# One subtraction moved behind another group, and one product split by halves of k instead of by columns, in a two-level fast matrix product

## The chip, the cores and the metric

The kernel runs on 1 core of one Trainium2 chip. The metric is device time in microseconds (us) for one execution. The kernel before takes 1524.74 us, the median of 3 runs (1524.18 to 1525.29).

Engines are named as in the profile: PE is TensorE (matmuls; PEld its weight loads), DVE is VectorE, ACT is ScalarE, POOL is GpSimd, SP is SyncE. L12 is line 12 of the kernel before.

## The reference

```python
m, k, n = 4096, 4096, 4096          # a, b, bias in float32
return np.tanh(np.matmul(a, b) + bias)
```

## The kernel before, in words

**Products.** The kernel does not multiply plainly. It works on items. An item is one column chunk `c` of 1024 columns (four chunks) and one pair of 128-row blocks of `a` (sixteen pairs). With the two row blocks, the two halves of k and the two halves of the chunk's columns, each item is a 2 x 2 by 2 x 2 block product, and seven products `m1` to `m7` stand in for eight: `m2 = s2 b11`, `m5 = s5 b22`, `m3 = a11 d3`, `m1 = s1 d1`, `m4 = a22 d4`, `m6 = s6 e6`, `m7 = s7 e7`. The left operands `s` are differences of quarters of `a` (`s6 = a21 - a11`, `s1 = a22 - a11`), the right operands `d` and `e` are sums and differences of quarters of `b`, all in fp16. A whole product is 16 matmuls (16 tiles of 128 along k) of 512 columns.

**Two levels.** In chunks 1 to 3, two items share a second level of the same idea: for a product such as m4, the two items' left operands, each cut into halves of k, are again a 2 x 2 block, and seven small products of 8 matmuls and 256 columns replace eight. The results of the small products are put together in PSUM by VectorE sums, with one ScalarE copy (`third`, L885) of a PSUM half to SBUF in between.

**The four-product order.** From some item on, chunks 2 and 3 treat two items `p` and `q` at a time in `four` (L992), which does m4, m2, m3 and one or two of m5 and m6 on two levels and m1, m7 whole. The order is written out by hand, and every engine takes its instructions in the order of the calls. For a pass that does not leave the order ("not leave"; `leave` is the last pass of chunk 2) TensorE's order is:

- m4 group 0, m2 group 0, m4 group 1, m2 group 1, m4 group 2, m2's products 7 and 3;
- m3 group 0, m2's product 4, x group 0, m3 group 1, x group 1, m3 group 2, x product 7 (x and y are m6 and m5, or m5 and m6);
- m1 of q, whole (16 matmuls of 512 columns);
- x products 3 and 4, y group 0;
- m1 of p, the columns 0 to 255 (16 matmuls, L1227);
- y group 1;
- m1 of p, the columns 256 to 511 (16 matmuls, L1230);
- y products 7 and 3, m7 of p, y product 4, m7 of q.

`group0` (L888), `group1` (L901) and `single` issue the small products through `multiply` (L868; the matmul is L879); `whole` (L935; the matmul is L939) issues a whole product. `group0` of m4 returns a function, called `w` in `four`, that does one VectorE sum: it adds the copy `x` of one PSUM half and another half into the place where m4's group 1 will accumulate. `group1` of m4 returns one that does two such sums, which m4's group 2 needs. `left` (L827) makes one small left operand on VectorE (128 x 1024), `four_sum` (L944) one whole left operand (128 x 2048); both end in `tt` (L144), so all VectorE arithmetic has line L144 in the profile. `seed` (L973) is a ScalarE copy of zeros into PSUM.

**Entering the order.** `turn_over` (L1311) runs once for chunk 2 and once for chunk 3, ahead of their first pass. It issues the last products of the two items before, while VectorE makes the first operands of the new pair `m`, `m + 1`. It ends with s6 of `m` (L1367), the last two products, s6 of `m + 1` (L1381) and one seed on ScalarE (L1383). Both s6 are written over a21. In later passes, `four` makes s6 of its items itself (L1087, L1112). The first use of the second item's s6 is the operand `v1` of m6, made after m2's products 7 and 3 (L1124).

**Right operands from memory.** Half-size right operands of m2 and m6 ("form") come back from device memory: each time TensorE has used one, `let_go` frees its tile and `pull_four` (L805) issues the next transfer on POOL's queue. Quarters of `a` are fetched on SP's queue.

Of the kernel before, what the change touches and what calls it, by code (L numbers as in the profile page):

```python
# [12 lines left out]
T = 16  # L13
TB = 4
TP = T // 2
# [87 lines left out]
HALF = (ds(0, NB // 2), ds(NB // 2, NB // 2))  # L103
# [10 lines left out]
def kernel(  # L114
# [28 lines left out]
    def tt(out_, in0, in1, op):  # L143
        nc.vector.tensor_tensor(out=out_, in0=in0, in1=in1, op=op)  # L144
# [6 lines left out]
    def bank(n, s, what):  # L151
        two = items[n][2] is not None
        if what == "w":
            return banks[5 + 2 * (n % 2)]
        if what == "z":
            return banks[4 + 2 * (n % 2) + (s if two else 0)]
        return banks[(0 if what == "d" else 2) + (s if two else n % 2)]
# [157 lines left out]
    def by_four(x):  # L315
        return x if len(x.shape) == 4 else x.rearrange("p (a b) m -> p a b m", b=TB)
# [507 lines left out]
    def half_of(n, what, h):  # L824
        return by_four(aset[n][TWO[what][0]])[:, ds(h * TP // TB, TP // TB)]

    def left(n, what, name):  # L827
        if what in FOURTH:
            left_of_four(n, what, name)
            return  # L830
        (i, h), (j, g) = {
            "s2": ((1, 0), (1, 1)), "s5": ((0, 1), (0, 0)), "s1": ((1, 1), (0, 0)),
            "s6": ((1, 0), (0, 0)), "s7": ((0, 1), (1, 1)),
        }[name]
        tt(by_four(place_for(what, name)), half_of(n + i, what, h), half_of(n + j, what, g), SUB)

    def place_for(what, name):
        k = left_count[0] % 4
        left_count[0] += 1
        owner[k] = what, name  # L840
        placed[what, name] = lefts[k]
        return lefts[k]

    def left_of_four(n, what, name):
        of = {"v2": "v1", "v4": "v2"}.get(name)
        if of:
            assert (what, of) in owner.values()
            of = by_four(placed[what, of])
        place = by_four(place_for(what, name))
        if name == "v1":  # L850
            tt(place, half_of(n + 1, what, 0), half_of(n + 1, what, 1), SUB)
        elif name == "v2":
            tt(place, half_of(n, what, 0), of, SUB)
        elif name == "v3":
            tt(place, half_of(n + 1, what, 0), half_of(n, what, 0), SUB)
        else:
            tt(place, half_of(n, what, 1), of, SUB)
# [30 lines left out]
    def group0(n, what, swapped=False):  # L888
        p, q = pair_of(n, what)
        if what in FOURTH:  # L890
            multiply(n, what, p[:, HALF[0]], (0, 0), (0, 0))
            nc.scalar.copy(p[:, HALF[1]], p[:, HALF[0]])
            multiply(n, what, between(n, what), "v1", "t1")
            return lambda: None
        parts = [(p[:, HALF[1]], "s5", (1, 1)), (q[:, HALF[0]], "s2", (0, 0))]
        for part in reversed(parts) if swapped else parts:
            multiply(n, what, *part)
        x = third(q[:, HALF[0]])
        return lambda: tt(between(n, what), x, p[:, HALF[1]], ADD)
# [32 lines left out]
        multiply(n, what, p[:, HALF[0]], "s7", "e7")  # L932
        multiply(n, what, q[:, HALF[1]], "s6", "e6")

    def whole(n, left_, right, parts=None, anew=False):  # L935
        at = by_four(aset[n][left_])
        for to, half in parts or ((bank(n, 0, "z"), ds(0, NB)),):
            for t in range(T):
                nc.tensor.matmul(  # L939
                    to[:, half], at[:, t // TB, t % TB], bop[right, t // TB][:, t % TB, half],  # L940
                    start=anew and t == 0, stop=t == T - 1, skip_group_check=True,
                )

    def four_sum(n, name, there):  # L944
        x, y = {
            "s2": ("a21", "a22"), "s5": ("a12", "a11"), "s1": ("a22", "a11"),
            "s6": ("a21", "a11"), "s7": ("a22", "a12"),
        }[name]
        st = aset[n]
        if there in QUADS:  # L950
            st[name] = st[there]
        elif there in "AB":
            st[name] = side[:, :, ds(NB * "AB".index(there), NB)].rearrange("p a (b m) -> p a b m", m=P)
        else:
            pool = {"wide": wide, "sum": sums, "spare": spare}.get(there, bops)
            st[name] = pool.tile([P, T, P], fp16, name=name, tag="sum" if there == "spare" else there)
        tt(by_four(st[name]), by_four(st[x]), by_four(st[y]), SUB)
# [29 lines left out]
    def more(calls):  # L987
        for f in left_over[:-(-len(left_over) // calls)]:
            f()
            left_over.pop(0)  # L990

    def four(n):  # L992
        c = items[n][0]
        p, q, m = n, n + 1, n + 2
        first, last = n == begins[c], m == len(items)
# [21 lines left out]
        def forms_at(k):  # L1017
            if first:
                m5_forms(k)

        def step(k):
            if leave:
                give_back(c, k)
# [12 lines left out]
        def take(what, i, later=False):  # L1036
            to = bank(i, 0, mine[what])
            if what == "m6":
                tt(st[i]["o"], st[i]["o"], to, ADD)
                ready = ("o", i, 1, 1)  # L1040
            else:
                tt(st[i]["ds"], st[i]["ds"], to, SUB)
                tt(st[i]["s"], to, st[i]["s"], ADD)
                ready = ("s", i, 0, 1)
            if later:
                left_over.append(lambda: end(*ready))
            else:
                end(*ready)
# [26 lines left out]
        left(n, "m2", "v2")  # L1075
        group0(n, "m2")
        left(n, "m4", "s7")
        more(3)
        step(1)
        w = group1(n, "m4")  # L1080
# [143 lines left out]
            fetch(m, "a22")  # L1224
            fetch(m + 1, "a22")
        forms_at(9)
        whole(p, "s1", "d1", ((bank(p, 0, "z"), HALF[0]),))  # L1227
        w, w2 = group1(n, y)
        take(x, q)
        whole(p, "s1", "d1", ((bank(p, 0, "z"), HALF[1]),))  # L1230
        if not last:
            fetch(m, "a11")
        w()
# [77 lines left out]
    def turn_over(c):  # L1311

        m = begins[c]
        p, q = m - 2, m - 1
        left_count[0] = 0
        del free[:]

        def slot(at):
            for f, args in work.pop(SLOTS * p + at, ()):
                if f in (put_four, put_sum, put_block):  # L1320
                    f(*args)

        queue.extend(
            (what, f) for n in range(m, ends_with[c], 2) for what in ("m2", "m6") for f in FOUR
            if what == "m2" or n + 2 in fours or c == NC - 1
        )
        free.extend(("b11_1", "b11_2", "b11_3"))
        for i in range(3):
            pull_four()
        aset[q]["s6"] = side[:, :, ds(0, NB)].rearrange("p a (b m) -> p a b m", m=P)  # L1330
        tt(aset[q]["s6"], by_four(aset[q]["a21"]), by_four(aset[q]["a11"]), SUB)
        asum(q, "s1")
        asum(q, "s7")
        fetch(m, "a22")
        fetch(m + 1, "a22")
        fetch(m, "a11")
        fetch(m + 1, "a21")
        slot(8)
        product(p, *PRODUCTS[8])
        fetch(m, "a21")  # L1340
        fetch(m + 1, "a11")
        product(q, *PRODUCTS[2])
        left(m, "m4", "s5")
        m5_forms(-7)
        slot(9)
        slot(10)
        twice(p, "m4", 2)
        left(m, "m4", "s2")
        seed(m, "d", 1)
        seed(m + 1, "d", 0)  # L1350
        m5_forms(-6)
        product(q, *PRODUCTS[5])
        slot(12)
        m5_forms(-5)
        four_sum(m, "s2", "sum")
        slot(13)
        product(p, *PRODUCTS[10])
        m5_forms(-4)
        seed(m, "z", 0)
        four_sum(m + 1, "s2", "sum")  # L1360
        left(m, "m2", "v1")
        seed(m, "c", 0)
        seed(m, "c", 1)
        slot(15)
        m5_forms(-3)
        if S6_AT == 0:
            four_sum(m, "s6", "a21")  # L1367
        product(q, *PRODUCTS[8])
        free.extend(("e6_2", "e6_3"))
        for i in range(2):  # L1370
            pull_four()
        slot(17)
        m5_forms(-2)
        if S6_AT == 1:
            four_sum(m, "s6", "a21")
        product(q, *PRODUCTS[10])
        free.append("sum")
        pull_four()
        if S6_AT == 2:
            four_sum(m, "s6", "a21")  # L1380
        four_sum(m + 1, "s6", "a21")  # L1381
        m5_forms(-1)
        seed(m + 1, "c", 0)  # L1383

# [219 lines left out]
    first = new_sum([P, 4, 4, TB * QP], fp16, "first")  # L1604
# [153 lines left out]
    for c in range(1, NC):  # L1758
        n = next(n for n in range(len(items)) if items[n][0] == c)
# [4 lines left out]
    for c in TWICE:  # L1764
# [31 lines left out]
        if c < NC - 1:  # L1796
            s1 = SLOTS * max(n for n in partner if items[n][0] == c)
# [43 lines left out]
    for slot in range(1 - len(ORDER), SLOTS * len(items)):  # L1841
# [14 lines left out]
        for pos, p in PRODUCTS.items():  # L1856
            n, r = divmod(slot - pos, SLOTS)
# [37 lines left out]
```

## Time and profile before

| | |
|---|---|
| median of the runs | 1524.74 us |
| profiled execution, device time | 1523.57 us |
| its span in the trace | 1521.9 us |
| granted TensorE clock | 1.00 |
| entry into the four-product order, chunk 2 / chunk 3 | about 928 us / 1251 us |
| passes that reach L1227 and L1230 | 3 in chunk 2, 6 in chunk 3 |

The profile is of one execution. Its span runs from the first to the last instruction; the device time also holds what lies around it. In a timeline row the columns are start and duration in us, engine, line, operation, output and inputs, and the number of instructions merged into the row; in brackets, how long the engine was idle before it and what released it. The matmuls are pipelined, so a row's duration holds the tail of its last matmul, and the distance from one row's start to the next row's start is what a step costs TensorE. The chain of waits follows the work that ended last back from the end; its rows give start, duration, engine and line.

### The profile page before, as it was taken

Reading aid. Unit: us, or ns where it says so; the run is one execution under the profiler, and the core shown is the slowest. Engines: PE = TensorE matmul, PEld = TensorE weight load, DVE = VectorE, ACT = ScalarE, POOL = GpSimd, SP = SyncE. Lnnn points to the kernel's source line nnn. Section 1 sums busy time; section 2 is a strip of 40 time slices with the busy share of each in tenths; the row PEclk is TensorE's granted clock in tenths of the full one; section 3 lists DMA queues with packets and bytes.
Section 4 is the critical chain, followed back from the end, with each engine's and each line's share of the span. In section 5 each row is a group of like instructions: output and inputs, shape, how many; then the busy total and the mean of one; then the engine's idle time right before and its main releaser. Section 6 shows DMA issues by size and latency. Waiting matters only on the chain.

```text
span 1521.9 us, 23593 instructions
## 1 busy us (share of the span) xinstructions
PE 1516.1 (100%) x8925; PEld 872.4 (57%) x8925; DVE 1238.9 (81%) x1671; ACT 347.6 (23%) x729; POOL 477.5 (31%) x868
## 2 busy tenths in 40 slices
PE   9999999999999999999999999999999999999999
PEld 4444444444445666544444557777644558878777
DVE  6789877777987777777798878988769979888887
ACT  4432111111221122111122112222122222223222
POOL 8775443333503231344560222111112211111110
PEclk9999999999999999999999999999999999999999
DMA  9999999999979998999996889889966789888884
GB/s 187 182 209 260 282 234 214 229 211 227 188 214 296 263 284 265 237 258 234 228 187 189 293 272 327 308 296 317 347 227 194 224 278 328 316 307 296 308 289 159
DMA packets 207254, 386.69 MB, mean 254 GB/s; under 512 B 25250, under 2 KB 104354, under 8 KB 207140
## 3 DMA queue, kind: packets, MB, share of 16 engines
q0 software_dynamic: 117232, 198.50, 56.6%
q1 hardware_dynamic: 89236, 186.36, 35.6%
q8 instruction: 70, 1.15, 0.3%
q10 hardware_dynamic: 672, 0.33, 0.1%
q14 instruction: 44, 0.36, 0.1%
HBM read 330.83 MB, written 139.98 MB: 309 GB/s over the span
## 4 chain that ended last, share of the span: by engine, by line
PE 99%; DVE 0%; DMA 0%; ACT 0%; issue 0%; DVEq 0%
PE ps L467 58%; PE ps L879 19%; PE ps L939 10%; PE ps L662 6%; PE ps L1540 5%; DMA coarse<-in_a_dram 0%; PE warm L1600 0%; DVE a L144 0%; PE spread L430 0%; PE tp L1641 0%; DVE form L144 0%; DVE h L144 0%; DVE o L144 0%; DVE first L1636 0%; DVE ps L144 0%; ACT ds L1269 0%
## 5 line engine op out<-in xcount | busy, mean ns | idle before, releaser
L467 PEld LDWEIGHTS <-s 128*128 128x128 f16 x2160 | 211.3, 98 | 249.6 <-DVE s L144 0.2
L467 PEld LDWEIGHTS <-a 128*128 128x128 f16 x1920 | 187.9, 98 | 223.5
L467 PE MATMUL ps<-b,s 128*128 128x512 f16 x1148 | 262.0, 379 | 0.0
L467 PE MATMUL ps<-e,a 128*128 128x512 f16 x908 | 206.9, 379 | 0.0
L467 PE MATMUL ps<-d,a 128*128 128x512 f16 x896 | 202.5, 379 | 0.0
L144 DVE TENSOR_TENSOR s<-a,a 128x2048 f16<-128x2048 f16 (+1 forms) x148 | 177.9, 1205 | 19.5 <-DMA a<-scratch 18.2
L269 DVE STREAM_TRANSPOSE a<-nat 128x1024 f16<-128x1024 f16 (+2 forms) x202 | 175.0, 910 | 9.8 <-PE ps L467 8.3
L879 PEld LDWEIGHTS <-h 128*128 128x128 f16 x1696 | 165.9, 98 | 24.8 <-DVE h L144 0.8
L811 POOL DMA_DIRECT2D form<-form_m x133 | 70.4, 529 | 348.5 <-PE ps L879 318.8
L467 PE MATMUL ps<-d,s 128*128 128x512 f16 x656 | 148.3, 379 | 0.0
L144 DVE TENSOR_TENSOR a<-a,a 128x2048 f16<-128x2048 f16 x120 | 145.7, 1215 | 0.0
L241 POOL DMA_DIRECT2D nat<-in_a_dram x176 | 93.0, 533 | 133.9 <-DVE a L269 63.4
L370 POOL DMA_DIRECT2D b<-in_b_dram x192 | 103.4, 545 | 82.5 <-DVE a L269 31.1
L879 PE MATMUL ps<-form,h 128*128 128x256 f16 x752 | 95.7, 273 | 0.0
L491 ACT ACTIVATE o<-ps 128x512 f32<-128x512 f32 x90 | 54.1, 601 | 163.2 <-issue 92.9
L939 PEld LDWEIGHTS <-a 128*128 128x128 f16 x608 | 58.9, 98 | 34.6
L879 PE MATMUL ps<-d,h 128*128 128x256 f16 x640 | 76.4, 273 | 0.0
L144 DVE TENSOR_TENSOR ps<-ps,x 128x256 f32<-128x256 f32 x126 | 53.8, 428 | 25.0 <-PE ps L879 10.0
L144 DVE TENSOR_TENSOR h<-a,a 128x1024 f16<-128x1024 f16 x108 | 71.5, 681 | 0.0
L939 PE MATMUL ps<-e,a 128*128 128x512 f16 (+2 forms) x320 | 68.8, 368 | 0.0
L662 PEld LDWEIGHTS <-h 128*128 128x128 f16 x600 | 58.7, 98 | 14.7
L879 PEld LDWEIGHTS <-a 128*128 128x128 f16 x600 | 58.7, 98 | 8.7
(186 smaller groups left out, 1933.5 us busy)
## 6 DMA issues: line engine op xcount, KB each, us to landing
a<-scratch SPq DMA_DIRECT2D x140, 512.0 KB, 5.5
form<-form_m POOLq DMA_DIRECT2D x133, 512.0 KB, 6.1
out_dram<-o SPq DMA_DIRECT2D x222, 256.0 KB, 5.6
nat<-in_a_dram POOLq DMA_DIRECT2D x288, 128.0 KB, 7.1
scratch<-a SPq DMA_DIRECT2D x48, 512.0 KB, 6.7
b<-in_b_dram POOLq DMA_DIRECT2D x160, 128.0 KB, 5.7
scratch<-a SPq DMA_DIRECT2D x32, 256.0 KB, 6.1
cast<-in_b_dram POOLq DMA_DIRECT2D x64, 128.0 KB, 9.0
```

Of the source, the lines that this page charges most:

```text
L144: nc.vector.tensor_tensor(out=out_, in0=in0, in1=in1, op=op)
L241: nc.gpsimd.dma_start(out=tl[ds(q * QP, QP), :, :], in_=src.rearrange("(mb p) k -> p mb k", p=QP),)
L269: nc.vector.transpose(dst[:, ds(b0 * tb, n * tb), :].rearrange("P (b t) (mb p) -> P mb b t p", t=tb, p=QP), src[:, :, ds(b0, n), :].rearra ...
L370: nc.gpsimd.dma_start(out=dst[ds(q * QP, QP), ds(t, nt)], in_=src)
L467: nc.tensor.matmul(st[where], at, bt, start=(what == "m2" or n < LEAD and what == "m1") and i == 0, stop=i == len(ts_) - 1, skip_group_che ...
L491: nc.scalar.activation(o, src, TANH)
L662: nc.tensor.matmul(to, at, bt, start=False, stop=t == TP - 1, skip_group_check=True)
L811: nc.gpsimd.dma_start(out=rights[what, name], in_=forms[what, name])
L879: nc.tensor.matmul(to, at, bt, start=False, stop=t == TP - 1, skip_group_check=True)
L939: nc.tensor.matmul(to[:, half], at[:, t // TB, t % TB], bop[right, t // TB][:, t % TB, half], start=anew and t == 0, stop=t == T - 1, skip ...
L1540: nc.tensor.matmul(mb[m % 4, j], aq[m, kt // T][:, kt % T, :], right(kt, j), start=fresh and kt == k0, stop=stop and kt == k1 - 1, skip_gr ...
```

## The change

Three edits in two functions. (1) `turn_over` no longer makes s6 of the second item. (2) The first pass of `four` makes it, after the second small operand that follows m4's group 0 and m2's group 0 and ahead of m4's group 1: `make("s6", q)` is the same `four_sum` over a21. (3) `whole` takes the tiles of k that it is to do, and the first item's m1 is cut at k instead of at the columns: the first 8 tiles of k over all 512 columns ahead of y's group 1, the other 8 behind it. `TP` is 8, `T` is 16.

```diff
-    def whole(n, left_, right, parts=None, anew=False):
+    def whole(n, left_, right, parts=None, anew=False, steps=range(T)):
         at = by_four(aset[n][left_])
         for to, half in parts or ((bank(n, 0, "z"), ds(0, NB)),):
-            for t in range(T):
+            for t in steps:
                 nc.tensor.matmul(
                     to[:, half], at[:, t // TB, t % TB], bop[right, t // TB][:, t % TB, half],
                     start=anew and t == 0, stop=t == T - 1, skip_group_check=True,
...
         left(n, "m4", "s7")
+        if first:
+            make("s6", q)
         more(3)
         step(1)
         w = group1(n, "m4")
...
         forms_at(9)
-        whole(p, "s1", "d1", ((bank(p, 0, "z"), HALF[0]),))
+        whole(p, "s1", "d1", steps=range(TP))
         w, w2 = group1(n, y)
         take(x, q)
-        whole(p, "s1", "d1", ((bank(p, 0, "z"), HALF[1]),))
+        whole(p, "s1", "d1", steps=range(TP, T))
...
             four_sum(m, "s6", "a21")
-        four_sum(m + 1, "s6", "a21")
         m5_forms(-1)
         seed(m + 1, "c", 0)
```

## The prediction, before the changed kernel was run

> **What bounds the kernel now.** I read the page's busy times and chain first, to see which engine sets the end.
>
> ```profile
> PE 1516.1 (100%) x8925; PEld 872.4 (57%) x8925; DVE 1238.9 (81%) x1671; ACT 347.6 (23%) x729; POOL 477.5 (31%) x868
> ...
> PE 99%; DVE 0%; DMA 0%; ACT 0%; issue 0%; DVEq 0%
> ```
>
> TensorE is busy in 1516.1 of 1521.9 us, and 99% of the chain that ends last is its matmuls. A change can therefore gain in two ways only: fewer matmul cycles, or one of the few places where TensorE stands still. The waits of TensorE, asked for by engine, name them all.
>
> ```profile
> PE warm L1600 <- DVE idle L405: 1.3, 1, 1.3
> PE ps L879 <- DVE ps L144: 0.9, 1, 0.9
> PE tp L1641 <- DVE first L1636: 0.5, 1, 0.5
> ```
>
> The first and the third belong to the opening. The second, one wait of 0.9 us in a `multiply` matmul (L879), is the only one in the part that the diff touches. Where it stands is seen in the timeline of TensorE around the second entry into the four-product order (column chunk 3):
>
> ```profile
> 1253.64 1.04 PE L879 MATMUL ps<-form,h 128*128 128x256 f16 x8
> 1255.54 1.03 PE L879 MATMUL ps<-g,h 128*128 128x256 f16 x8 [0.87 <-DVE ps L144]
> 1256.41 1.91 PE L879 MATMUL ps<-g,a 128*128 128x256 f16 x16
> ...
> 1259.90 1.91 PE L879 MATMUL ps<-d,h 128*128 128x256 f16 x16
> ```
>
> The row at 1253.64 is the last of m2's first group, 1255.54 is the first of m4's second group, 1259.90 is m4's third group. Eight 256-wide matmuls take a slot of 0.87 (1255.54 to 1256.41), so without a wait the second group would start at 1253.64 + 0.87 = 1254.51. It starts 1.03 later; that is the loss, as a start-to-start time. VectorE's timeline there shows what came between:
>
> ```profile
> 1252.73 0.68 DVE L144 TENSOR_TENSOR o<-ds,ps 128x512 f32<-128x512 f32 x1
> 1253.33 1.22 DVE L144 TENSOR_TENSOR a<-a,a 128x2048 f16<-128x2048 f16 x1
> 1254.46 0.68 DVE L144 TENSOR_TENSOR h<-a,a 128x1024 f16<-128x1024 f16 x1
> 1255.07 0.42 DVE L144 TENSOR_TENSOR ps<-x,ps 128x256 f32<-128x256 f32 x1
> 1255.40 0.68 DVE L144 TENSOR_TENSOR h<-s,h 128x1024 f16<-128x1024 f16 x1
> 1256.00 1.28 DVE L144 TENSOR_TENSOR h<-a,a 128x1024 f16<-128x1024 f16 x2
> 1258.43 0.90 DVE L144 TENSOR_TENSOR ps<-ps,x 128x256 f32<-128x256 f32 x2 [1.14 <-PE ps L879]
> ...
> 1260.11 0.69 DVE L144 TENSOR_TENSOR h<-s,h 128x1024 f16<-128x1024 f16 x1 [0.19 <-PE ps L879]
> ```
>
> The 128x2048 row at 1253.33 is the second item's s6, the step that the change moves. Behind it stand m4's s1 (1254.46) and the sum that closes m4's first group (1255.07); when that ends at 1255.49, TensorE goes on 0.05 later. After two differences (v2 is 1255.40, s7 and s6 of m4 are the pair at 1256.00) VectorE waits 1.14 us for TensorE.
>
> **The moved subtraction.** It is one VectorE instruction per entry, two in the kernel. It issues no DMA, and the changed kernel's instruction order shows POOL, ACT and SP untouched. Its slot is 1254.46 - 1253.33 = 1.13. Taken from its old place, m4's s1 would run 1253.33 to 1254.01. But the sum at 1255.07 reads `x`, which ScalarE copies out of PSUM, and that copy is late next:
>
> ```profile
> 1253.44 0.63 ACT L565 ACTIVATE o<-o 128x512 f32<-128x512 f32 x1 [2.66 <-DVE o L144]
> 1253.98 0.36 ACT L973 CAST ps<-zeros 128x256 f32<-128x256 f16 x1
> 1254.28 0.36 ACT L885 COPY x<-ps 128x256 f32<-128x256 f32 x1
> ...
> 1285.71 0.38 ACT L885 COPY x<-ps 128x256 f32<-128x256 f32 x1
> ```
> ```profile
> 1286.13 0.43 DVE L144 TENSOR_TENSOR ps<-ps,x 128x256 f32<-128x256 f32 x1 [0.25 <-ACT x L885]
> ```
>
> ScalarE waits for `o` (1252.73 on VectorE, ahead of the moved step and so not earlier after the change), then does a tanh, a seed and the copy, which ends at 1254.64. The last two rows, later in the pass, show the delay from such a copy's end (1286.09) to its sum on VectorE (1286.13): 0.04. So: sum 1254.68 to 1255.10, TensorE 0.05 later at 1255.15 instead of 1255.54. The gain is 0.39, not 1.03; 0.64 of the stall stays, with ScalarE's copy behind it.
>
> The first entry (chunk 2) is the same order 323 us earlier. TensorE, then VectorE, then ScalarE:
>
> ```profile
> 930.89 1.04 PE L879 MATMUL ps<-form,h 128*128 128x256 f16 x8
> 931.83 1.03 PE L879 MATMUL ps<-g,h 128*128 128x256 f16 x8
> ```
> ```profile
> 931.36 0.42 DVE L144 TENSOR_TENSOR ps<-x,ps 128x256 f32<-128x256 f32 x1
> ...
> 932.29 1.28 DVE L144 TENSOR_TENSOR h<-a,a 128x1024 f16<-128x1024 f16 x2
> 934.72 0.90 DVE L144 TENSOR_TENSOR ps<-ps,x 128x256 f32<-128x256 f32 x2 [1.14 <-PE ps L879]
> ```
> ```profile
> 930.58 0.36 ACT L885 COPY x<-ps 128x256 f32<-128x256 f32 x1
> ```
>
> Here the group starts 931.83 - (930.89 + 0.87) = 0.07 late. The copy ends at 930.94, the sum could end at 930.98 + 0.42 = 931.40, before TensorE is ready at 931.76: all of the 0.07 goes. Together the removal is worth 0.39 + 0.07 = 0.46 us.
>
> At its new place the step stands between m4's s7 and s6. It takes along its wait for the fetched a21 and a11; at 1253.33 it showed no idle time, so that data is there, and it is asked for about 3 us later. Queued behind it are m4's s6 and the two sums at 1258.43. In chunk 3: v2 from 1255.01, s7 1255.61, the step 1256.21, m4's s6 1257.34, done about 1258.02. TensorE, 0.39 earlier, lets the sums go at 1258.43 - 0.39 = 1258.04. It fits, with almost nothing over: the 1.14 of idle time is filled by 1.13. In chunk 2 about 0.3 is over (0.01 + 0.38 - 0.07), because there the sum starts 0.38 earlier but TensorE only 0.07. If the cover were gone, the first to suffer is m4's third group, which needs the first of the sums: 1258.04 + 0.42 = 1258.46 against 1259.90 - 0.39 = 1259.51, a margin of 1.05. Further down, 0.19 of idle time at 1260.11 takes up a small delay. I take the new place at 0.
>
> **m1 of the first item.** Before, 2 x 16 matmuls of 256 columns; after, 2 x 8 of 512, in the same two places, around y's second group. Only the non-leaving passes reach this line. Groups of L939 by form, and the weight loads at that line:
>
> ```profile
> L939 PE MATMUL ps<-d,a 128*128 128x256 f16 x288 | 34.4, 273 | 0.0
> ```
> ```profile
> L939 PEld LDWEIGHTS <-a x608: 97/98/98, 957.9 to 1518.5; 128*128 128x128 f16 x152
> ```
>
> 288 / 32 gives nine passes. The group's busy time merges overlaps, so the length is taken from the chain, one pass of chunk 3:
>
> ```profile
> 1274.91 3.45 PE ps L939 x16
> 1278.37 3.49 PE ps L879 x32
> 1281.86 1.75 PE ps L939 x16
> 1283.61 1.75 PE ps L879 x16
> 1285.35 1.75 PE ps L939 x16
> 1287.10 1.75 PE ps L879 x16
> 1288.85 3.45 PE ps L939 x16
> ```
>
> 16 matmuls of 512 columns (m1 of the second item, m7) take 3.45, or 0.216 each. 32 of 256 columns take 3.49 (the L879 row), 0.109 each. So a pass goes from 3.49 to 3.45, 0.04 less (0.03 to 0.05 by the rounding). Nine passes: 0.36 us. 144 weight loads go as well, but a load of 98 ns lies beside a matmul of 109 and costs nothing already.
>
> The row is not what the Trainium skill gives, page "TensorE: Matmul & The Clock Gate", section "Back-to-back issue gap": pairs of a weight load and a matmul in a real kernel space at about 131 ns for 512 columns and 81 for 128. An estimate from that page, 98 at 256 on a straight line, makes 32 x 98 - 16 x 131 = 1.04 us a pass, 9.4 in all. The trace disagrees: 216 ns at 512 columns.
>
> What m1's halves cover shrinks with them, by 0.018 each. The closest dependants, on VectorE:
>
> ```profile
> 1280.00 1.22 DVE L144 TENSOR_TENSOR a<-a,a 128x2048 f16<-128x2048 f16 x1
> ...
> 1286.47 0.68 DVE L144 TENSOR_TENSOR h<-side,h 128x1024 f16<-128x1024 f16 x1
> ```
> ```profile
> 1281.70 1.91 PE L939 MATMUL ps<-d,a 128*128 128x256 f16 x16
> ```
>
> The first is m1's own s1, which ends at 1281.22, 0.48 before m1's first half. The second is y's v4, which ends at 1287.15; its matmuls come after three stretches of 1.75 and a slot of 0.87, at 1287.82: 0.67 to spare. No wait appears. No reader of PSUM is new either: the bank that m1 now writes whole from the start was last read by the two `ds` sums ahead of m3's second group.
>
> **The sum.** 0.39 + 0.07 + 0.36 = 0.82 us. The profiled execution took 1523.57 (span 1521.9 and 1.67 around it), so it would become 1522.75. It lies 1.17 under the median of the three runs, 1524.74; against that median the forecast is 1523.92 us, 0.05% less. A measurement of this kernel tells about 0.2% (3.05 us) from no change, so this is "no change".
>
> **The rivals.**
> *The whole stall goes*: 1.03 + 0.07 + 0.36 = 1.46, 1523.3 us. It needs ScalarE's copy 0.6 earlier than its rows allow; nothing before it moves. 0.10.
> *The entry gains nothing*, because something else releases m4's second group, or the filled gap (1.13 into 1.14) gives back what was won: only m1's 0.36 is left, 1524.4 us. For it: the fit has no reserve in chunk 3. Against: the 1.05 of margin behind. 0.14. That the edit fails to move the step is out: the instruction order shows it after m4's s7 in both entries.
> *Slower: changing width costs a slot.* After the change TensorE goes 256, 512, 256, 512, 256 columns around m1, four seams a pass, 36 in all, where now all is 256. If each seam lost one 256-wide slot, 0.109, that is 3.92, and 3.92 - 0.82 = 3.10 on top: 1527.8 us. It decides from 0.82 / 36 = 23 ns a seam. Against: m1 of the second item has both seams now, and its neighbours still start 3.45 apart with 16 x 0.216. 0.04.
> *Wide matmuls nearly free.* If a 512-wide matmul were held by its weight load alone, 98 ns, a pass would lose 3.49 - 1.57 = 1.92, nine 17.3, with the entries' 0.46 17.7: 1507.0 us. The chain's 3.45 for 16 speaks flatly against it. [...] 0.02.
>
> **How the numbers follow.** Forecast 0.70, the others 0.10, 0.14, 0.04, 0.02. Predicted 1523.92. Range: the three runs spread over 1.11 and lie up to 0.56 from their median; the lowest of the first three cases less 0.56 is 1522.7, the highest (1524.4) plus a whole spread 1525.5. It leaves out the two rivals of 0.06 and some scatter. Within 0.2%: 0.94; faster 0.02; slower 0.04.
>
> **What would show it.** In the new profile TensorE's wait at the second entry should shrink by 0.39, to about 0.5, and its VectorE sum should name ScalarE's `x` as releaser; at the first entry the sum should also wait for that copy. VectorE's 1.14 before the two sums should shrink to under 0.1 in chunk 3 and about 0.3 in chunk 2. L939 should hold 144 matmuls `ps<-d,a` of 512 columns at 1.73 per half in the chain, with no idle time. I am wrong if TensorE shows a new wait after either entry, if halves of m1 take other than 1.73, or if waits on DMA appear that no row here has.

## The result, and the profile after

The changed kernel takes 1523.00 us (median of 22 runs, 1521.95 to 1525.29), the kernel before 1525.28 beside it (22 runs, 1524.17 to 1527.47). The ratio is 0.9986, 95% interval 0.9980 to 0.9993. It is faster by 2.3 us at the median and by 1.1 to 3.1 us by the interval; that is 0.14%, less than the 0.2% that the forecast took as "no change". The time lies in the forecast range, but the forecast gain was 0.82 us, little more than a third of the measured one. So it is the width of the range that holds it, and the three runs behind the forecast had a median 0.54 us under that of all 22.

The profiled execution took 1522.73 us (span 1521.0), 0.84 less than that of before. That is almost the forecast, and it is so by luck, as the terms show. First TensorE at the second entry (chunk 3), in the profile after:

```profile
1253.86 1.04 PE L879 MATMUL ps<-form,h 128*128 128x256 f16 x8
1254.94 1.03 PE L879 MATMUL ps<-g,h 128*128 128x256 f16 x8
```

m4's second group starts 1254.94 - (1253.86 + 0.87) = 0.21 late, instead of 1.03. VectorE there, same profile:

```profile
1252.51 0.68 DVE L144 TENSOR_TENSOR o<-ds,ps 128x512 f32<-128x512 f32 x1
1253.10 0.69 DVE L144 TENSOR_TENSOR h<-a,a 128x1024 f16<-128x1024 f16 x1
1254.45 0.43 DVE L144 TENSOR_TENSOR ps<-x,ps 128x256 f32<-128x256 f32 x1 [0.67 <-ACT x L885]
1254.79 0.68 DVE L144 TENSOR_TENSOR h<-s,h 128x1024 f16<-128x1024 f16 x1
1255.39 0.68 DVE L144 TENSOR_TENSOR h<-a,a 128x1024 f16<-128x1024 f16 x1
1256.00 1.22 DVE L144 TENSOR_TENSOR a<-a,a 128x2048 f16<-128x2048 f16 x1
1257.13 0.68 DVE L144 TENSOR_TENSOR h<-a,a 128x1024 f16<-128x1024 f16 x1
1257.83 0.90 DVE L144 TENSOR_TENSOR ps<-ps,x 128x256 f32<-128x256 f32 x2
```

The moved subtraction is the row at 1256.00. Without it, m4's s1 is done at 1253.79, and the closing sum still waits 0.67 for ScalarE's `x`. The 1.14 of idle time before the two sums is filled, with nothing over. The quantity to read is the distance from the start of the `o` subtraction to TensorE's start: 1254.94 - 1252.51 = 2.43; before it was 1255.54 - 1252.73 = 2.81. That is 0.38 less. The stall shrank by 0.82, and the other 0.44 has nothing to do with the moved row: `o` now starts 1253.86 - 1252.51 = 1.35 ahead of TensorE's row, where it was 1253.64 - 1252.73 = 0.91 before. Where this comes from is seen under the experiments. At the first entry (chunk 2), TensorE and then VectorE:

```profile
930.88 1.04 PE L879 MATMUL ps<-form,h 128*128 128x256 f16 x8
932.18 1.03 PE L879 MATMUL ps<-g,h 128*128 128x256 f16 x8 [0.26 <-DVE ps L144]
```
```profile
924.94 0.69 DVE L144 TENSOR_TENSOR o<-ds,ps 128x512 f32<-128x512 f32 x1 [3.18 <-DMA out_dram<-o]
...
929.75 0.68 DVE L144 TENSOR_TENSOR o<-ds,ps 128x512 f32<-128x512 f32 x1
```

932.18 - 929.75 is 2.43 again, yet this entry lost time: it stalls 0.43, where the profile before had 0.07. The reason stands in the first VectorE row. The first of the two `o` subtractions waited for an earlier output's transfer, because it needs a free output tile, and everything behind it runs without a gap: 4.81 us from it to the second `o`. In the profile before the same row was released by TensorE and came 0.72 earlier:

```profile
924.22 0.69 DVE L144 TENSOR_TENSOR o<-ds,ps 128x512 f32<-128x512 f32 x1 [2.58 <-PE ps L467]
```

m1, in the chain of waits after, one pass of chunk 3:

```profile
1277.76 3.49 PE ps L879 x32
1281.26 1.73 PE ps L939 x8
1282.98 1.75 PE ps L879 x16
1284.73 1.73 PE ps L939 x8
1286.46 1.75 PE ps L879 x16
1288.20 3.45 PE ps L939 x16
```

8 matmuls of 512 columns take 1.73, and the 256-wide groups around them still 1.75: no seam. So the 0.84 between the two profiles is +0.36 at the first entry, -0.82 at the second and -0.36 for m1, to 0.02. The forecast had -0.07, -0.39 and -0.36 for them.

### The profile page after: what moved, and what is told of

The parts are those of the page before. It is cut to its first block, busy times and chain, and to the rows that moved or that the text cites. A ratio compares the mean times of both kernels' runs of the same rounds, so it can differ in the third digit from the quotient of the medians.

```text
span 1521.0 us, 23305 instructions
## 1 busy us (share of the span) xinstructions
PE 1515.6 (100%) x8781; PEld 855.7 (56%) x8781; DVE 1239.0 (81%) x1671; ACT 347.5 (23%) x729; POOL 477.7 (31%) x868
## 3 DMA queue, kind: packets, MB, share of 16 engines
q8 instruction: 69, 1.13, 0.3%
## 4 chain that ended last, share of the span: by engine, by line
PE 99%; DMA 0%; DVE 0%; ACT 0%; issue 0%; DVEq 0%
PE ps L467 58%; PE ps L879 19%; PE ps L939 10%; PE ps L662 6%; PE ps L1541 5%; DMA coarse<-in_a_dram 0%; PE warm L1601 0%; PE spread L430 0%; DVE form L144 0%; PE tp L1642 0%; ACT o L565 0%; DVE o L144 0%; DVE ps L144 0%; DVE first L1637 0%; ACT x L885 0%
## 5 line engine op out<-in xcount | busy, mean ns | idle before, releaser
L467 PEld LDWEIGHTS <-a 128*128 128x128 f16 x1920 | 187.3, 98 | 224.1 <-DVE a L269 0.5
L939 PEld LDWEIGHTS <-a 128*128 128x128 f16 x464 | 44.7, 98 | 44.7
L879 PEld LDWEIGHTS <-a 128*128 128x128 f16 x600 | 58.6, 98 | 9.1
```

Of the source, the lines that this page charges most:

```text
L467: nc.tensor.matmul(st[where], at, bt, start=(what == "m2" or n < LEAD and what == "m1") and i == 0, stop=i == len(ts_) - 1, skip_group_che ...
L879: nc.tensor.matmul(to, at, bt, start=False, stop=t == TP - 1, skip_group_check=True)
L939: nc.tensor.matmul(to[:, half], at[:, t // TB, t % TB], bop[right, t // TB][:, t % TB, half], start=anew and t == 0, stop=t == T - 1, skip ...
```

## The experiments

The question became what an entry costs in other executions. This table holds, for each profile, the start-to-start stall of m4's second group at both entries and, in brackets, the distance from the `o` subtraction to TensorE. It is worked out as above; where there is no stall, the distance is only what TensorE's own pace gives. "Outputs in place" is the run that takes a transfer's wait away.

| version | chunk 2 | chunk 3 |
|---|---|---|
| before, first profile | 0.07 (2.80) | 1.03 (2.81) |
| before, again | 2.01 (2.81) | 1.37 (2.81) |
| m1 alone, two profiles | 0.71 (2.81), 0.50 (2.81) | 0.40 (2.81), 0.44 (2.81) |
| late tanh alone | 1.01 (2.81) | 1.38 (2.81) |
| outputs in place | 0 | 1.30 (2.80) |
| subtraction doubled, old place | 1.66 (4.07) | 2.94 (4.07) |
| changed kernel | 0.43 (2.43) | 0.21 (2.43) |
| moved subtraction alone | 0 | 0.68 (2.44) |
| subtraction doubled, new place | 0 | 0 |
| both moves and late tanh, m1 at the columns, two profiles | 0, 0 | 0, 0 |
| both moves and late tanh, m1 at k, two profiles | 0, 0.08 | 0, 0 |

**The parts by themselves.** m1 alone, the edits of `whole` and its two calls and nothing else:

```diff
-        whole(p, "s1", "d1", ((bank(p, 0, "z"), HALF[0]),))
+        whole(p, "s1", "d1", steps=range(TP))
...
-        whole(p, "s1", "d1", ((bank(p, 0, "z"), HALF[1]),))
+        whole(p, "s1", "d1", steps=range(TP, T))
```

> The kernel before with the edit of m1 alone (halves of k). Theory A (the edits act on the path only through the rows of the two profiles): nine passes lose 0.04 us each, 0.36 us faster than before, ratio about 0.9998, within scatter; L939 has 8 matmuls per half at 1.73; the wait of TensorE at the two entries stays what the kernel before has, and its size differs from the first profile (0.07 and 1.03 as start-to-start) because it follows when transfers land. Theory B (the split gains more than the rows show): 1 us or more faster.

Measured: 1523.28 against 1524.93, ratio 0.9989 (0.9980 to 0.9998). The rows of m1 are those of theory A, but the time fell by more, 1.65 us; the interval's end is just what A says. Repeated on another chip:

> m1 alone once more, on another chip, since its first run gave 0.9989 where the rows give 0.9998. Theory A: nearer to 0.9998, as the entries keep the old order and scatter by 1 us; the span from m4's second group of chunk 3 to the end is 0.24 shorter than before's. Theory B: 0.9989 again.

Measured: 1524.17 against 1525.05, 0.9994 (0.9985 to 1.0003). That is 0.88 us, between the two theories, with an interval that holds both. The stall at the second entry is 0.40 and 0.44 in the two profiles, less than in any other profile with the subtraction in its old place. The moved subtraction alone:

```diff
         left(n, "m4", "s7")
+        if first:
+            make("s6", q)
...
-        four_sum(m + 1, "s6", "a21")
```

> The kernel before with the moved subtraction alone. Theory A: 0 to 0.38 us for each of the two entries, at most 0.76 us faster, ratio 0.9995 to 1.0000; in the profile the sum that releases m4's second group waits for ScalarE's copy of x, 2.43 us from the start of the last o subtraction to TensorE's start wherever there is a stall. Theory C (the entries of an ordinary execution lose more than the profiled ones, and the whole slot of 1.13 comes back at each): about 2 us faster, ratio 0.9985 or less.

Measured: 1524.04 against 1524.93, 0.9994 (0.9985 to 1.0003): 0.9 us, near A's upper end of 0.76. The 2.44 at the second entry is A's number; theory C's whole slot does not come back.

**The kernel before, once more.**

> The kernel before, unchanged: what the comparison itself scatters, and a second profile of the two entries. Theory A: ratio 1.000 within 0.0005; the start-to-start stalls at the entries differ from 0.07 and 1.03 by some tenths, because the VectorE chain ahead of them is released by a transfer (2.81 us from the start of the last o subtraction to TensorE's start in both). Rival: the stalls come back as the same numbers, so the landing of transfers plays no part.

Measured: 1525.50 against 1524.93, 1.0003 (0.9994 to 1.0012). The stalls did not come back as the same numbers: 2.01 and 1.37 instead of 0.07 and 1.03, 2.3 us more, in a span of 1525.5 instead of 1521.9; of the rest, about 0.7 came ahead of the first entry and about 0.7 between the two. The distance of 2.81 is the same to 0.01. VectorE at the first entry of that profile:

```profile
923.85 1.23 DVE L144 TENSOR_TENSOR s<-a,a 128x2048 f16<-128x2048 f16 x1 [4.38 <-DMA a<-scratch]
926.83 0.69 DVE L144 TENSOR_TENSOR o<-ds,ps 128x512 f32<-128x512 f32 x1 [1.75 <-DMA out_dram<-o]
...
931.63 0.68 DVE L144 TENSOR_TENSOR o<-ds,ps 128x512 f32<-128x512 f32 x1
```

Two transfers release VectorE one after the other, and 4.80 later stands the `o` that starts the 2.81.

**Taking the transfer away.** The two results ahead of an entry are made in place of `ds`, so no output tile is waited for:

```diff
-                o = st["ds"] if n + 2 == plain else new_out()
+                o = st["ds"] if n + 2 == plain or begins.get(c) in (n + 1, n + 2) else new_out()
```

> The kernel before, but the last two m7 results ahead of each entry are made in place of ds, so they need no free output tile and VectorE no longer waits there for an earlier result's transfer to the output. Theory A (the landing of transfers sets the stall of an entry, and by it much of the scatter): in chunk 2 the o subtraction is released by TensorE, as in the first profile, and the stall there is 0.07 whatever the transfers do; the other profiles of the old order had 2.01, 0.71 and 1.01, so the median falls by 0.5 to 1.3 us. Chunk 3, where VectorE waits for the staged form's transfer, keeps its stall of 0.4 to 1.4. Rival (the stall follows something else): chunk 2 still stalls by 0.5 or more, ratio 1.000.

Measured: 1524.19 (1523.48 to 1525.06) against 1525.05 (1523.51 to 1527.05), 0.9995 (0.9987 to 1.0004). The median falls by 0.86, as theory A said, though the interval does not exclude none. The profile does show it. VectorE, with the last subtraction now called `ds`:

```profile
929.43 0.69 DVE L144 TENSOR_TENSOR ds<-ds,ps 128x512 f32<-128x512 f32 x1 [2.02 <-PE ps L467]
```

TensorE releases it, and the stall of chunk 2 is 0.00. Chunk 3 keeps one of 1.30. With the transfer's wait the stall of chunk 2 was 0.50 to 2.01 in the four profiles of the old order that show it; without it, it was 0.07 and 0.00 in two. So the landing of a transfer sets that stall, as far as one profile of this run can show it.

**Doubling the subtraction.** One more of the same size, its result unused, at the old place:

```diff
+        tt(side[:, :, ds(0, NB)].rearrange("p a (b m) -> p a b m", m=P), by_four(aset[m + 1]["a21"]), by_four(aset[m + 1]["a11"]), SUB)
         four_sum(m + 1, "s6", "a21")
```

> The kernel before, with one more subtraction of the same size at the old place of the second item's s6, its result unused. Theory A: VectorE's chain to the entry grows by one slot of 1.13, so 3.94 us from the last o subtraction to TensorE's start, and each entry that stalls is 1.13 later: 2.0 to 2.3 us slower than before, ratio 1.0013 to 1.0015. Rival (the old place was not on the path in an ordinary execution): 1.000.

Measured: 1528.63 against 1525.32, 1.0017 (1.0009 to 1.0026). The distance is 4.07, so the added slot cost 1.26, not 1.13, at both entries: 2.5 us of the 3.3. The old place is on the path. The same at the new place, ahead of `make("s6", q)`:

> The changed kernel, with one more subtraction of the same size at the new place, its result unused. By the rows of the changed kernel VectorE would then be 1.1 late at the two sums of m4's second group in chunk 3 and 0.8 in chunk 2, where m4's third group leaves 1.05 and the first item's s1 0.48 plus 0.19 of idle time: about 0.1 us of stall ahead of m4's third group and 0.1 to 0.4 ahead of m1's first half, 0.5 us slower than the changed kernel in all, ratio near 0.999. Rival 1 (the new place is covered twice over): no difference. Rival 2 (the new place is on the path): 1.13 at each entry, 2.3 slower, as slow as before or slower.

Measured: 1523.63 against 1525.32, 0.9991 (0.9983 to 1.0000), so about 0.8 us slower than the changed kernel by the two ratios, though their intervals overlap. TensorE, then VectorE at the first entry:

```profile
935.35 1.04 PE L879 MATMUL ps<-form,h 128*128 128x256 f16 x8
936.82 1.91 PE L879 MATMUL ps<-d,h 128*128 128x256 f16 x16 [0.43 <-DVE ps L144]
```
```profile
935.88 0.89 DVE L144 TENSOR_TENSOR ps<-ps,x 128x256 f32<-128x256 f32 x2
```

m4's third group now starts 0.60 late (0.54 in chunk 3), where 0.1 was expected. The sums end at 935.88 + 0.89 = 936.77, TensorE starts 0.05 later: it waits for both sums, not for the first alone. Ahead of m1 nothing stalls. The new place is thus covered once, by the idle time it fills, and not twice.

**What holds the rest of the stall.** ScalarE's copy of `x` stands behind a tanh that waits for the last `o`. Here that tanh and its store are called after the copy:

```diff
                 tt(o, st["ds"], st["z"], SUB)
-                nc.scalar.activation(o, o, TANH)
-                store(o, pair, 0, c, 0)
+                def close():
+                    nc.scalar.activation(o, o, TANH)
+                    store(o, pair, 0, c, 0)
+                if begins.get(c) == n + 1:
+                    left_over.append(close)
+                else:
+                    close()
```

> The changed kernel, and besides the last tanh and store ahead of each entry are issued behind the entry's copy of x on ScalarE. If that copy is what still holds the entry (theory A), the stalls left in the changed kernel's profile (0.42 and 0.20 as start-to-start) go, so about 0.6 us faster than the changed kernel, 1.7 us faster than before if the entries are as in the profiles; no wait of TensorE at L879 is left. Rival: the sum is held by VectorE's own work (m4's s1), then the stall stays as it is.

Measured: 1522.55 (1522.23 to 1523.05) against 1524.93, 0.9984 (0.9975 to 0.9992). No stall is left at either entry. The same edit without the moved subtraction:

> The kernel before, with only the last tanh and store ahead of each entry moved behind the entry's copy of x. Theory A: the sum still stands behind s6 and s1 on VectorE, so ScalarE's earlier copy buys nothing: ratio 1.0000 within the scatter, 2.81 us from the start of the last o subtraction to TensorE's start in both entries that stall. Rival (ScalarE alone holds the entry): as fast as the version with both moves, 0.9987.

Measured: 1525.24 against 1525.32, 0.9996 (0.9987 to 1.0005), and 2.81 at both entries. Each of the two chains, VectorE's and ScalarE's, hides the other: moving the tanh alone shortens the distance by nothing, moving the subtraction alone by 0.38.

**m1's cut without the entries' noise.**

> The version with the moved subtraction and the late tanh, but m1 of the first item cut at the columns as before. With no stall left at the entries, this shows m1's cut by itself. Theory A: nine passes of 3.49 instead of 3.45, so 0.36 us slower than the version with both (which ran 1522.55, ratio 0.9984), that is ratio 0.9986 to 0.9988 and a median near 1522.9. Theory B (the cut at k is worth more than its rows, as the run of m1 alone with 0.9989 could mean): 1.3 us or more slower than the version with both, ratio 0.9993 or more.

Measured: 1523.17 against 1525.32 on another chip, 0.9986 (0.9977 to 0.9995). Side by side on one chip:

> The version with both moves at the entry and m1 cut at the columns, beside the same with m1 cut at k on the same chip. Theory A: no stall at either entry, little scatter, and 0.36 us between the two medians. Theory B: 1.3 us or more between them.

> The version with both moves and m1 cut at k, for the comparison above, and a second run against before: 0.998 to 0.999, no wait of TensorE at the entries.

Measured: 1523.34 with the columns (0.9991, 0.9982 to 0.9999) and 1522.78 with k (0.9985, 0.9976 to 0.9994). The medians differ by 0.56, nearer to 0.36 than to 1.3. The waits of TensorE in the second:

```profile
PE warm L1607 <- DVE idle L405: 1.3, 1, 1.3
PE tp L1648 <- DVE first L1643: 0.6, 1, 0.6
PE ps L1547 <- DVE oa L269: 0.4, 1, 0.4
```

Only the opening is left; the 0.08 in the table is under what this view lists. This version is faster than the kernel before, and its 22 runs on two chips lie between 1522.23 and 1523.45, while before's 33 on either chip spread over 3.5 us or more. Against the changed kernel its lead is not shown: 0.9984 and 0.9985 beside 0.9986, with intervals that overlap.

**m1's cut at the second entry.** The profiles hold one effect more. TensorE's last row of m2's first group in chunk 3 starts 0.26 to 0.92 after the second `o` subtraction in all eight profiles with m1 at the columns, and 1.35 to 1.76 after it in all six with m1 at k. The ranges do not meet, whatever else was changed, so at this entry m1's cut brings VectorE earlier. In 13 of the 14 profiles VectorE's last wait ahead of it ends with the transfer of a staged right operand to memory, `form_m<-stage`. In the kernel before, and then with m1 alone:

```profile
1240.86 0.70 DVE L144 TENSOR_TENSOR ps<-cs,ps 128x512 f32<-128x512 f32 x1 [0.19 <-PE ps L467]
...
1246.72 1.29 DVE L144 TENSOR_TENSOR stage<-e,stage 128x1024 f16<-128x1024 f16 x2 [1.91 <-DMA form_m<-stage]
```
```profile
1242.37 0.70 DVE L144 TENSOR_TENSOR ps<-cs,ps 128x512 f32<-128x512 f32 x1 [0.18 <-PE ps L467]
...
1247.59 1.29 DVE L144 TENSOR_TENSOR stage<-e,stage 128x1024 f16<-128x1024 f16 x2 [1.71 <-DMA form_m<-stage]
```

From the row that TensorE releases to the row behind the transfer it is 5.86 in the first and 5.22 in the second; over all profiles 5.80 to 6.50 at the columns and 5.02 to 5.42 at k. The stall with the subtraction in its old single place follows: 1.03, 1.37, 1.38 and 1.30 at the columns, 0.40 and 0.44 at k, so about 0.85 less. With the 0.36 of its rows the cut is worth about 1.2 us on the old order, and the two runs of m1 alone gained 1.65 and 0.88. Where no stall is left to shorten, only the 0.36 remains.

The traces offer a cause. A 16 KB transfer on queue q8, which the DMA view calls `instruction`, takes about 0.95 us and starts 0.2 to 0.7 after the TensorE-released row in all eight profiles at the columns, while `form_m<-stage` is under way. In the six at k it starts 7.8 to 8.9 after that row, behind the landing. The three passes of chunk 2 have 96 TensorE instructions fewer at k, 16 matmuls and 16 weight loads each, which would move a transfer of code so. No run moved that transfer by itself, so this cause is argued and not shown.

## Why the prediction was right, and where not

- **The path.** Right. TensorE bounds the kernel, and only the entry's stall and m1's cycles were to be had.
- **ScalarE's copy is late next.** Right: 0.39 expected, 0.38 measured (2.81 to 2.43), with the sum released by `x`. The rivals "the whole stall goes" and "the entry gains nothing" both fell.
- **The first entry, 0.07.** Here the size failed. It was read from one execution, in which TensorE happened to release VectorE; in the four others of the old order in which a transfer releases it, the stall is 0.50 to 2.01. There the move is worth the whole 0.38 too. So two of the prediction's signs of being wrong came up in the profile after, a wait of TensorE (0.26) and one on a DMA (`out_dram<-o`) at this entry; the second profile of the kernel before shows both as well, so the change did not bring them. The entries' term is up to 0.76, not 0.46, and the sum up to 1.12, not 0.82.
- **The new place at nothing.** Right in effect. Its margin of 1.05 was wrong: TensorE waits for the second sum, and the doubled subtraction cost 0.57 an entry. The 0.3 that was to be left over in chunk 2 is not there either, since this entry stalled as the second one did.
- **m1, 0.36.** Right for the matmuls' own time: from m4's second group in chunk 2 to the second entry the changed kernel takes 0.13 less, from m4's second group in chunk 3 to the end 0.24 less, and the chain's halves are 1.73. But the prediction put everything else about the cut at nothing, and that failed: at the second entry the cut takes about 0.85 off the stall of the old order. The rivals on seams and on nearly free wide matmuls fell. The 131 ns that the Trainium skill gives for 512 columns (page "TensorE: Matmul & The Clock Gate", section "Back-to-back issue gap") is not met here: 8 in 1.73 us are 216 ns each.
- **What stays open.** With m1's effect at the second entry the profiles account for up to 1.8 us: 1.06 at the second entry (1.27 as a mean of the four stalls at the columns, 0.21 in the changed kernel), up to 0.38 at the first, 0.36 in m1's rows. That lies in the measured interval of 1.1 to 3.1; its middle, 2.3, is 0.5 more. At the first entry, what comes ahead of the `o` subtraction is the same in all versions, so I take the luck of the transfers to be part of the rest. That was not shown. Why the staged transfer lands earlier with m1 at k was not tested either.

## What to carry to other kernels

Where a stall ends in a rigid chain released by a transfer, one profile gives the chain's length well and the stall badly: read the distance from the releasing instruction, not the idle time. Before crediting a step taken off a chain, find what is late next on the other engine; here two chains of nearly one length had to be shortened together. The best result is then less scatter as much as less time. And compare that distance over many versions: an edit far from a stall, here m1's cut, can shift the transfer that releases it.

## What the runs showed of the hardware

At the first entry, where the code up to it is the same, the stall was 0.07 to 2.01 us in five profiles of the old order, while distances inside an engine's chain repeated to 0.01 us. At the second entry, VectorE's row behind a 512 KB transfer came 5.80 to 6.50 us after a row released by TensorE in the eight profiles with a 16 KB `instruction` transfer beside it, and 5.02 to 5.42 us after it in the six without; that the one delays the other is not shown. A doubled VectorE subtraction of 1.22 us cost a slot of 1.26 behind it, where the single one takes 1.13. Matmuls of 512 columns beside groups of 256 kept their pace on both sides: 8 in 1.73 us between groups of 16 in 1.75 us.
